# A Mamba mixer's groups: C computed a group ahead, states times C and gate sums on VectorE, the first z columns beside dt

## The chip, the cores and the metric

The kernel runs on one core of one Trainium2 chip. The metric is the device time of one execution in microseconds (us). The engines are named as in the profile: PE is TensorE (PEld its weight loads), DVE VectorE, ACT ScalarE, POOL GpSimd, and SP SyncE, which issues the DMAs. A name such as "SPq" means the instruction queue of that engine.

## The reference

One step of a decoder layer for 256 prompt tokens and 8 sample tokens, which bring their own recurrent states. All of it is float32.

```python
h = h + 0.5 * rmsnorm(swiglu(rmsnorm(h)))          # FFN 1
mix = token_mixer(rmsnorm(h))                      # the part that is changed
h = h + rmsnorm(mix)
h = h + 0.5 * rmsnorm(swiglu(rmsnorm(h)))          # FFN 2
h = h + rmsnorm(sigmoid(rmsnorm(h) @ w_ple_gate) * (p @ w_ple_proj))

def token_mixer(u):
    glu_a, glu_b, z, xbc, dt = split(u @ w_in)     # 1024, 1024, 3072, 5120, 48 columns
    v = silu(layernorm(dwconv31(glu_a * sigmoid(glu_b))))
    x, B, C = split(silu(dwconv4(xbc)))            # 3072, 8 x 128, 8 x 128
    dt = softplus(dt + dt_bias)                    # 48 heads, 6 in each of 8 groups
    a_cs = cumsum(dt * a)                          # per chunk of 128 tokens
    y = (C . B * exp(a_cs[l] - a_cs[s])) @ (x * dt)   # within a chunk
      + exp(a_cs) * (C @ state)                    # from the state before
      + d_skip * x
    y = y * silu(z)
    y = y * rsqrt(mean over the group's 384 columns of y * y + eps) * ssm_norm_g
    return concat(v, y) @ w_out                    # and the new states
```

For a sample token the chunk is that one token, so `C @ state` is the product of its own state, 128 numbers for each of 64 x 48 rows, with C, summed over the 128.

## The kernel before, in words

Columns of a projection lie on 128 partitions, the 264 tokens along the free axis. Each float32 weight is split into a high and a low part in TensorE's fast float32 form, and so is each activation; a 128 x 128 weight tile then gives three matmuls of 128x264 into one accumulator: high x high, high x low, low x high (`mm3`, L250 to L252).

**Weights** stream in units of up to 16 tiles (48 matmuls), in the order of a table (`PLAN`). A unit comes in two halves of eight tiles, 512 KB each. Per half, SP issues the load of `wraw` (L153), ACT casts it to `whi` (L154), and DVE subtracts to get `wlo` (L155). Each of the three tiles has four buffers, so two units; a half of unit n + 2 can be made only once PE has finished that half of unit n. A column unit of the input projection is one such unit: 128 output columns.

**The mixer's input projection** runs over 81 column units (`IN_ORDER`): first `dt`, then for each of 8 groups B, C, x0, (in four groups a pair for the GLU), x1, x2, z0, z1, z2. The first four units are computed together, so they end at one time.

After each B, C or x unit comes `do_conv`: a width-4 convolution on DVE (STTs, L219) and a SiLU on ACT (L243). After `dt`, `do_dt` writes dt and dt x a of the samples to memory (`d_dt`) and loads them back repeated over the partitions (`dtp`, `eap`), takes the exponential of `eap`, forms the running sums with matmuls and writes them to memory (`d_cs`).

`decays(g)`, at x0, loads the group's running sums from `d_cs` twice (`ab`, `ea`, L702 and L710) and makes the decays with 12 Relus and 3 exponentials on ACT. `ssd(g)`, at x2, does the scan of the group: PE transposes x and B (L727, L728), forms C . B (L741), the states (L753), the products within a chunk (L768) and from the state (L775). Then, for the samples, it transposes B and C (L781, L782), copies them to `rows` on ACT (L784), writes `d_bc`, loads C back repeated over all partitions as `cbc` (L787), and for each of the 3 x 2 pieces of the sample states loads `h0` (128 x 512, L792), multiplies it by `cbc` on GpSimd and sums it over the last axis on DVE (L794). GpSimd also scales the first chunk's state by `cd`.

`gate(g)`, at x0 of the next group, multiplies y by SiLU(z) and forms the sum of squares with `SumSq`: ACT squares, GpSimd adds (`run`), and a matmul with ones (L306) sums over the partitions. `L216` and `L219` are helpers for DVE and GpSimd operations, `L243` that for ACT's.

The order of the instructions on each engine is set by a scheduler when the program is built; each engine then works through its own in that order, and waits for the others at semaphores. The memory tiles `d_bc`, `d_cs` and `d_dt` make a write and a load that depends on it go through SP's queue one behind the other.

```python
rows = mp.tile([P, 2, P], F32, tag="rows", bufs=1, name=nm("rows"))
cbc = mp.tile([P, NS, P], F32, tag="cbc", bufs=1, name=nm("cbc"))
h0 = mp.tile([P, 4, P], F32, tag="h0", bufs=3, name=nm("h0"))
ab: bufs=2, one for each chunk;  ea: bufs=1
```

## Time and profile before

| | |
|---|---|
| median of 3 runs | 2429.63 us (2427.08 to 2433.99) |
| the profiled execution, its own time | 2432.44 us |
| its span | 2430.7 us |
| mean granted clock of TensorE | 0.993 |
| busy share PE, DVE, ACT, POOL | 97%, 65%, 49%, 12% |
| the mixer's input projection | about 820 to 1362 us of the span |
| bytes read from memory | 465.65 MB |

A row of the wait view reads: engine, tile and line that waited `<-` what it waited for: total us, times, longest. A row of the group view reads: line, engine, operation, out`<-`in, shapes, count | busy us, mean ns of one | idle time of the engine before them and what ended it. A row of the timeline or of the chain of work that ended last begins with start and duration; in square brackets is the idle time before it.

### The profile page before, as it was taken

The numbers are of one execution on the slowest core, as the hardware profiler recorded it, in microseconds if no ns is written. First come the engines' busy times: TensorE is split into PE (matmuls) and PEld (weight loads), VectorE is DVE, ScalarE is ACT, GpSimd is POOL, SyncE is SP. The second block draws the span as 40 slices with busy tenths as digits, with TensorE's granted clock in tenths as the row PEclk, the third lists the DMA queues.
The fourth block names the chain that finished last, engine by engine and source line by source line (L and its number), as shares of the span: only waits on it lengthen the run. The fifth ranks groups of instructions, "written<-read, shape, count | busy, mean of one in ns | idle before, by whom it ended". The sixth has DMA issues, their size and how long they took to land.

```text
span 2430.7 us, 47409 instructions
## 1 busy us (share of the span) xinstructions
PE 2367.7 (97%) x19448; PEld 2342.7 (96%) x19448; DVE 1569.2 (65%) x2333; ACT 1181.4 (49%) x1771; POOL 298.4 (12%) x295
## 2 busy tenths in 40 slices
PE   8999999999999889999999999999999999999988
PEld 8999999999999889999999999999999999999988
DVE  6554455545557858988798975766545565565585
ACT  6444444433456465665565545544444443344465
POOL 0400000000015212122122010101000000000103
PEclk9999999999999999999999999999999999999999
DMA  7655555555556666666666556476766776676553
GB/s 249 217 183 184 182 183 182 183 183 183 183 169 207 213 180 193 207 216 202 210 216 205 181 181 216 153 238 228 240 213 223 237 236 217 217 236 206 184 191 132
DMA packets 166250, 489.89 MB, mean 202 GB/s; under 512 B 25568, under 2 KB 42640, under 8 KB 166032
## 3 DMA queue, kind: packets, MB, share of 16 engines
q1 hardware_dynamic: 166032, 486.86, 62.0%
q8 instruction: 152, 2.49, 0.4%
q14 instruction: 66, 0.54, 0.1%
HBM read 465.65 MB, written 22.42 MB: 201 GB/s over the span
## 4 chain that ended last, share of the span: by engine, by line
PE 84%; DVE 6%; issue 3%; ACT 3%; DMA 2%; POOL 1%; SPq 0%; ACTq 0%; POOLq 0%; DVEq 0%
PE acc L250 27%; PE acc L251 27%; PE acc L252 27%; DVE wlo L155 2%; DVE y L219 1%; ACT whi L154 1%; PE ps L306 1%; DVE h L216 1%; DMA ab<-d_cs 1%; DMA cbc<-d_bc 1%; DVE ych L794 1%; PE ps L250 0%; ACT tmp L243 0%; DMA d_bc<-rows 0%; PE ps L251 0%
## 5 line engine op out<-in xcount | busy, mean ns | idle before, releaser
L252 PE MATMUL acc<-act,wlo 128*128 128x264 f32 x6224 | 1770.7, 285 | 4.3 <-DVE wlo L155 4.1
L251 PE MATMUL acc<-act,whi 128*128 128x264 f32 x6224 | 1756.6, 283 | 6.3 <-DVE act L216 6.2
L250 PE MATMUL acc<-act,whi 128*128 128x264 f32 x6224 | 1747.7, 283 | 3.4 <-DVE tmp L216 2.1
L155 DVE TENSOR_TENSOR wlo<-wraw,whi 128x1024 fp32r<-128x1024 f32 (+2 forms) x812 | 986.9, 1217 | 597.9 <-ACT whi L154 595.5
L154 ACT CAST whi<-wraw 128x1024 fp32r<-128x1024 f32 (+2 forms) x812 | 829.9, 1026 | 961.9 <-PE acc L251 717.3
L250 PEld LDWEIGHTS acc<-act,whi 128*128 128x128 f32 x6224 | 1175.5, 190 | 6.0 <-issue 2.1
L251 PEld LDWEIGHTS acc<-act,whi 128*128 128x128 f32 x6224 | 1169.2, 188 | 9.9 <-DVE act L216 7.9
L252 PEld LDWEIGHTS acc<-act,wlo 128*128 128x128 f32 x6224 | 1167.9, 188 | 8.3 <-DVE wlo L155 6.4
L216 POOL TENSOR_TENSOR run<-run,tmp 128x264 f32<-128x264 f32 x93 | 87.8, 944 | 962.9 <-ACT tmp L243 961.8
L216 POOL TENSOR_TENSOR s<-s,eap 128x1024 f32<-128x1024 f32 x24 | 48.8, 2035 | 630.4 <-DMA s<-in_hst 630.4
L219 DVE SCALAR_TENSOR_TENSOR y<-v,vec,y 128x251 f32<-128x251 f32 (+23 forms) x240 | 118.1, 512 | 1.2
L219 DVE SCALAR_TENSOR_TENSOR s<-bb,xds,s 128x128 f32<-128x128 f32 x192 | 52.7, 346 | 66.1 <-POOL s L216 66.1
L216 POOL TENSOR_TENSOR h<-h,cbc 128x512 f32<-128x512 f32 x48 | 73.6, 1553 | 166.0 <-DMA cbc<-d_bc 90.9
L258 ACT CAST act<-tmp 128x264 fp32r<-128x264 f32 x120 | 48.7, 410 | 69.9 <-DVE tmp L216 55.2
L216 DVE TENSOR_TENSOR tmp<-acc,rr 128x264 f32<-128x264 f32 x100 | 43.0, 430 | 51.0 <-PE acc L252 50.8
L216 DVE TENSOR_TENSOR tmp<-tmp,acc 128x264 f32<-128x264 f32 x86 | 36.7, 427 | 38.7 <-PE acc L252 38.6
L216 DVE TENSOR_TENSOR act<-tmp,act 128x264 fp32r<-128x264 f32 x120 | 56.1, 471 | 0.3
L243 ACT ACTIVATE tmp<-tmp 128x264 f32<-128x264 f32 x112 | 47.0, 420 | 8.7 <-DVE tmp L216 8.4
L243 ACT ACTIVATE tmp<-y 128x264 f32<-128x264 f32 x67 | 28.0, 425 | 44.1 <-DVE y L216 43.0
L216 DVE TENSOR_TENSOR y<-y,acc 128x264 f32<-128x264 f32 x80 | 34.0, 425 | 24.0 <-PE acc L252 24.0
L794 DVE TENSOR_REDUCE ych<-h 128x4 f32<-128x512 f32 x48 | 32.4, 678 | 17.5 <-POOL h L216 17.5
L250 PE MATMUL ps<-act,whi 128*128 128x264 f32 x96 | 28.4, 304 | 15.4 <-ACT whi L154 8.1
(165 smaller groups left out, 926.1 us busy)
## 6 DMA issues: line engine op xcount, KB each, us to landing
wraw<-in_w SPq DMA_DIRECT2D x756, 512.0 KB, 4.7
h<-in_hst SPq DMA_DIRECT2D x48, 256.0 KB, 3.9
s<-in_hst SPq DMA_DIRECT2D x24, 512.0 KB, 6.5
out_nss<-s SPq DMA_DIRECT2D x24, 512.0 KB, 3.0
wraw<-in_w SPq DMA_DIRECT2D x24, 384.0 KB, 4.1
wraw<-in_w SPq DMA_DIRECT2D x32, 256.0 KB, 3.9
ab<-d_cs SPq DMA_DIRECT2D x16, 384.0 KB, 5.1
cbc<-d_bc SPq DMA_DIRECT2D x8, 512.0 KB, 4.3
```

The lines of the kernel that those rows point to most:

```text
L154: nc.scalar.copy(hi, raw)
L155: nc.vector.tensor_tensor(out=lo, in0=raw, in1=hi.bitcast(F32), op=ALU.subtract)
L216: return (eng or nc.vector).tensor_tensor(out=out, in0=in0, in1=in1, op=op)
L219: return nc.vector.scalar_tensor_tensor(out=out, in0=in0, scalar=scalar, in1=in1, op0=op0, op1=op1)
L243: i = nc.scalar.activation(out=out, in_=in_, func=func, bias=bias, scale=scale)
L250: nc.tensor.matmul(acc, hi, x[:, 0, :], start=first, stop=False)
L251: nc.tensor.matmul(acc, hi, x[:, 1, :], start=False, stop=False)
L252: return nc.tensor.matmul(acc, lo, x[:, 0, :], start=False, stop=last).ins
L258: nc.scalar.copy(t[:, 0, :], x)
L306: nc.tensor.matmul(p, ones, s, start=i == 0, stop=i == len(self.parts) - 1)
L794: nc.vector.tensor_reduce(out=ych[:, j, b : b + 4], in_=h0, op=ALU.add, axis=AX.X)
```

## The change

It rearranges the mixer.

- The first four units are dt, z0, z1, z2 of group 0 (before: dt, B, C, x0). C of a group is computed in the group before it, behind x2. Group 0 runs z0, z1, z2, C0, B0, x0, x1, x2, C1; a later group B, x0, (pair), x1, x2, C of the next, z0, z1, z2.
- `do_dt` is split in four: `do_dt`, `do_sums` (at B of group 0), `do_exps` and `load_dt` (at x1). The exponential of dt x a is taken on 48 x 8 before the write instead of on the loaded, repeated 128 x 192.
- `load_sums` (loads of `ab`, `ea`) comes at B, the decays' ACT work at x1, tied behind the cast of the last weight half issued so far. `decay_cb` (C . B and its product with the decays) moves from x2 to x1.
- B and C each have a `b` and `c` tile and their own transposed copy to memory (`to_memory`), through a `rows` tile with one buffer, half the size.
- `h0` is one piece of 128 x 1024 (512 KB) per column tile, with two buffers. Its product with `cbc` and the sum run on DVE, one product and one reduce for each tile, tied behind the last weight subtract issued so far; at x0, x1, x2 of groups 2 to 7, and one unit later in groups 0 and 1.
- The product of the state with `cd` and the gate's additions run on DVE. The gate is split: `gate_begin` at B of the next group, `gate_end` with the matmul total at x0, tied behind the last matmul issued so far.
- The tiles `btm` and `cb` are taken from the `rr` tiles.

`tc.issue_after(i)` sets what follows behind instruction i in the order.

```diff
+        z = [("z", MT_Z + 3 * g + j) for j in range(3)]
+        if g == 0:
+            out.extend(z)
+            out.append(("C", MT_CM))
         out.append(("B", MT_BM + g))
-        out.append(("C", MT_CM + g))
         out.append(("x", MT_X + 3 * g))
         if g in GLU_IN:
             pair()
         out.extend(("x", MT_X + 3 * g + j) for j in (1, 2))
-        out.extend(("z", MT_Z + 3 * g + j) for j in range(3))
+        if g + 1 < GRP:
+            out.append(("C", MT_CM + g + 1))
+        if g:
+            out.extend(z)
...
+    def do_exps(dta):
+
+        act(dte, dte, AF.Exp)
+        act(cd, cd, AF.Exp)
+        ed = mp.tile([P, NS], F32, name="ed")
+        act(ed[:NH], dta[:, NP_:], AF.Exp)
+        nc.sync.dma_start(d_dt[1], ed[:NH])
...
-        act(eap, eap, AF.Exp)
...
+    def decays(g):
+
+        ab, ea = sums.pop(g)
+        with tc.issue_after(ws.hi):
+            for c, t in enumerate(ab):
+                for h in range(HPG):
+                    i = HPG * g + h
+                    act(t[:, h, :], t[:, h, :], AF.Relu, bias=acs[:, c, i : i + 1], scale=-1.0)
+                act(t, t, AF.Exp, scale=-1.0)
+            act(ea, ea, AF.Exp)
         return ab, ea
+
+    def to_memory(g, i, t):
+
+        pr = ps_tile([P, P])
+        nc.tensor.transpose(pr[:NS], t[:, NP_:], ident)
+        rows = mp.tile([P, P], F32, tag="rows", bufs=1, name=nm("rows"))
+        nc.scalar.copy(rows[:NS], pr[:NS])
+        nc.sync.dma_start(d_bc[g, i], rows[:NS])
+
+    def load_cbc(g):
+        cbcs[g] = mp.tile([P, NS, P], F32, tag="cbc", bufs=1, name=nm("cbc"))
+        with tc.issue_after(ws.dma.ins):
+            nc.sync.dma_start(cbcs[g], d_bc[g, 1].partition_broadcast(P))
+
+    def load_state(g, j):
+        h0s[g, j] = mp.tile([P, NS, P], F32, tag="h0", bufs=2, name=nm("h0"))
+        with tc.issue_after(ws.dma.ins):
+            nc.sync.dma_start(h0s[g, j], a["hst"][3 * g + j])
+
+    def state_times_c(g, j):
+
+        if not j:
+            ychs[g] = mp.tile([P, 3, NS], F32, tag="ych", bufs=1, name=nm("ych"))
+        h0 = h0s.pop((g, j))
+        with tc.issue_after(ws.lo):
+            tt(h0, h0, cbcs[g], ALU.mult)
+            nc.vector.tensor_reduce(out=ychs[g][:, j, :], in_=h0, op=ALU.add, axis=AX.X)
...
-                tt(s, states[0], cd[:, hs].unsqueeze(2).to_broadcast([P, HPG, 64]), ALU.mult, nc.gpsimd)
+                tt(s, states[0], cd[:, hs].unsqueeze(2).to_broadcast([P, HPG, 64]), ALU.mult)
...
-        for j in range(3):
-            for b in range(0, NS, 4):
-                h0 = mp.tile([P, 4, P], F32, tag="h0", bufs=3, name=nm("h0"))
-                nc.sync.dma_start(h0, a["hst"][3 * g + j][:, b : b + 4, :])
-                tt(h0, h0, cbc[:, b : b + 4, :], ALU.mult, nc.gpsimd)
-                nc.vector.tensor_reduce(out=ych[:, j, b : b + 4], in_=h0, op=ALU.add, axis=AX.X)
...
+    def gate_begin(g, y, zs):
+
         tt(y, y, zs, ALU.mult)
-        sq = SumSq(3, direct=0)
+        sq = SumSq(3, direct=0, eng=nc.vector)
         for j in range(3):
             sq.add(y[:, j, :])
+        return g, y, sq
+
+    def gate_end(g, y, sq):
+
         t = tmp()
-        rsqrt(t, sq.total(), eps1, 1.0 / 384)
+        rsqrt(t, sq.total(traced[0]), eps1, 1.0 / 384)
...
```

Three places where the order of instructions moves follow. A row there has the line, the operation, what it writes and reads, and the shape; the last number of a name is that of the tile.

TensorE at the gate total between groups 2 and 3, before: the total (L306) over `run`, and the transposes of x0 (L727), behind the first matmul of x1's unit.

```order
L252 MATMUL acc_12452<-act_9315,wlo_8_12336 128x264
L250 MATMUL acc_12514<-act_9201,whi_0_12392 128x264
L306 MATMUL ps_12035<-run_12026,ones 128x264
L727 MATMUL ps_12218<-ident,h_12017 128x128
L727 MATMUL ps_12227<-ident,h_12017 128x128
L251 MATMUL acc_12514<-act_9201,whi_0_12392 128x264
```

The same place after the change: the total (L316) stands behind all 48 matmuls of the unit `acc_12376`, which began with `wlo_0_12158`'s half, and C . B (L779) and the transposes (L795) follow it.

```order
L261 MATMUL acc_12376<-act_9315,wlo_8_12164 128x264
L316 MATMUL ps_12040<-run_11944,ones 128x264
L779 MATMUL ps_12146<-c_11656,b_11935 128x128 x2
L795 MATMUL ps_12229<-ident,h_12026 128x128
L261 MATMUL acc_12441<-act_9201,wlo_0_12304 128x264
```

What moved: the total's input `run` is now made on DVE, and the total is the first of the small matmuls there.

DVE in a group's second unit, before: the reduces (L794) of the state products stand one by one between convolution steps and weight subtracts (L155).

```order
L155 TENSOR_TENSOR wlo_8_11965<-wraw_8_11963,whi_8_11964 128x1024
L219 SCALAR_TENSOR_TENSOR bc_11874<-acc_11886,vec,bc_11874 128x253
L794 TENSOR_REDUCE ych_11574<-h_622_11579 128x4
L219 SCALAR_TENSOR_TENSOR h_12017<-acc_11956,vec,h_12017 128x255
L216 TENSOR_TENSOR h_12017<-h_12017,shist 128x8
L219 SCALAR_TENSOR_TENSOR y_11352<-v_11346,vec,y_11352 128x232
L794 TENSOR_REDUCE ych_11574<-h_623_11583 128x4
L155 TENSOR_TENSOR wlo_0_12080<-wraw_0_12078,whi_0_12079 128x1024
```

After, at the head of group 3 (`h_11518` is y, `h_11734` SiLU(z), `h_647` and `h_648` are sample states):

```order
L162 TENSOR_TENSOR wlo_8_12069<-wraw_8_12067,whi_8_12068 128x1024
L226 SCALAR_TENSOR_TENSOR y_11342<-v_11336,vec,y_11342 128x237
L223 TENSOR_TENSOR h_11518<-h_11518,h_11734 128x792
L223 TENSOR_TENSOR h_647_11959<-h_647_11959,cbc_11736 128x1024
L223 TENSOR_TENSOR h_648_11961<-h_648_11961,cbc_11736 128x1024
L226 SCALAR_TENSOR_TENSOR y_11342<-v_11336,vec,y_11342 128x236
L772 TENSOR_REDUCE ych_12034<-h_647_11959 128x8
L772 TENSOR_REDUCE ych_12034<-h_648_11961 128x8
L226 SCALAR_TENSOR_TENSOR y_11342<-v_11336,vec,y_11342 128x235
L226 SCALAR_TENSOR_TENSOR h_12026<-acc_12060,vec,h_12026 128x255
L223 TENSOR_TENSOR h_12026<-h_12026,shist 128x8
L162 TENSOR_TENSOR wlo_0_12158<-wraw_0_12156,whi_0_12157 128x1024
```

What moved: two products and two whole reduces stand together between two weight halves, and the first product reads `cbc_11736`. Right behind the last row comes the gate's addition, `run_11944`. SP's rows that bring this `cbc` (C's rows are `rows_11666`, B's of the group before `rows_11577`):

```order
L724 DMA ab_11953<-d_cs 128x6x128
L160 DMA wraw_0_12156<-in_w 128x1024
L751 DMA d_bc<-rows_11577 8x128
L727 DMA ea_11956<-d_cs 64x3x128 x2
L160 DMA wraw_8_12162<-in_w 128x1024
L751 DMA d_bc<-rows_11666 8x128
L758 DMA cbc_11736<-d_bc 128x1024
```

Before, there was one write of both (8x2x128), and the load of `cbc` behind it.

ACT in group 0, before: the exponential of the loaded `eap` stands ahead of the SiLUs of B, C (`bc`) and x0 (`h_9644`).

```order
L618 COPY tmp_9624<-ps_9621 48x256
L243 ACTIVATE eap<-eap 128x192
L243 ACTIVATE dte<-dte 128x96
L243 ACTIVATE cd<-ps_9612 128x48
L238 ACT_TABLE_LOAD
L243 ACTIVATE bc_9627<-bc_9627 128x264 x2
L243 ACTIVATE h_9644<-h_9644 128x264
```

After: the exponential is that of `ed`, 48 x 8; the Relus on the loaded `ab` stand between the casts of two halves of one weight unit.

```order
L250 ACTIVATE cd<-cd 128x48
L250 ACTIVATE ed<-h_9584 48x8
L161 CAST whi_8_9859<-wraw_8_9858 128x1024
L655 COPY xo_9667<-acc_9851 128x11
L250 ACTIVATE h_9836<-acc_9851,vec 128x264
L161 CAST whi_0_9961<-wraw_0_9960 128x1024
L250 ACTIVATE ab_9844<-ab_9844,acs 128x128 x6
L250 ACTIVATE ab_9845<-ab_9845,acs 128x128 x6
L161 CAST whi_8_9967<-wraw_8_9966 128x1024
```

What moved: ACT's wait for a load in this group is now that for `ab`, with the cast of a weight half behind it. SP's order there is: the write of `d_bc` (C's rows of group 0), a weight half, `cbc` load, a weight half, the write of `d_cs`, that of `d_dt`, then the loads of `ab`.

## Prediction

> **What bounds the kernel now.** I read the page's busy shares first, then busy time by stage, then TensorE's waits in the one stage that the change touches.

> ```profile
> PE 2367.7 (97%) x19448; PEld 2342.7 (96%) x19448; DVE 1569.2 (65%) x2333; ACT 1181.4 (49%) x1771; POOL 298.4 (12%) x295
> 200.00:700.00 500.00, 500.00 (x4169) 500.00 (x4168) 252.51 (x272) 204.78 (x246) 0.00 (x0) 1.00 0.58 182
> 820.00:1362.00 542.00, 517.17 (x4205) 499.84 (x4205) 441.95 (x759) 314.36 (x579) 99.91 (x75) 0.99 0.64 200
> ```

> TensorE is the bound. In the first FFN it never stops: 4169 matmuls in 500 us, 0.120 us each, so a unit of 48 takes 5.76 us (about 5.9 in the mixer with its small matmuls). In the mixer's input projection (820 to 1362 us; the columns are span, PE, PEld, DVE, ACT, POOL, granted clock, DMA share, GB/s) it is busy for 517 of 542 us, and DVE for 442. The change leaves TensorE's work as it is, so it can only win what TensorE loses here: idle time and clock.

> ```profile
> PE ps L306 <- POOL run L216: 11.8, 8, 2.6
> PE ps L727 <- ACT h L243: 7.3, 2, 4.9
> PE acc L252 <- DVE wlo L155: 4.1, 8, 0.9
> PE ps L753 <- ACT btm L736: 1.1, 1, 1.1
> ```

> These are TensorE's waits between 820 and 1362 us (total, times, longest). The eight gate totals wait for GpSimd's sum of squares, two stops come in group 0, and the late low halves of weights cost 4.1. Lost clock comes on top:

> ```profile
> 863.11 0.69 PE L727 MATMUL ps<-ident,h 128*128 128x128 f32 x2 [4.90 <-ACT h L243]
> 875.87 0.64 PE L727 MATMUL ps<-ident,h 128*128 128x128 f32 x3 [2.43 <-ACT h L243]
> 857.00:868.00 11.00, 6.10 (x39) 5.89 (x39) 1.59 (x3) 7.12 (x15) 0.00 (x0) 0.84 0.68 197
> 868.00:880.00 12.00, 9.57 (x66) 9.25 (x66) 9.15 (x15) 10.69 (x22) 0.00 (x0) 0.86 0.43 135
> 918.00:930.00 12.00, 9.43 (x64) 9.11 (x63) 8.32 (x16) 8.13 (x16) 2.95 (x2) 0.86 0.64 217
> ```

> The three windows around the 4.9, the 2.43 and the longest gate wait (2.6) show clocks of 0.84, 0.86 and 0.86: 0.16 x 11 + 0.14 x 12 + 0.14 x 12 = 5.1 us lost, 1.7 behind each gap.

> **The change, part by part.** The sum is made against the profiled execution, 2432.44 us (span 2430.7 and 1.7 around it). That one lies 2.8 above the median of the three runs, 2429.63, so 2.8 comes off at the end.

> *Gate totals, -11.8 and -1.7 of clock.* The sums of squares go to DVE one unit earlier, and the total is issued at the end of x0's unit. In the order shown, the last addition stands right behind `wlo_0_12158` on DVE, while TensorE has all 48 matmuls of that half's unit (5.8 us) ahead of the total. If the sum were late, the weights ahead of it would be later still. I take the whole wait as gone. What is late next at that place are the weights, priced below.

> *Group 0, -7.3 and -3.4 of clock, +4.7 back.*

> ```profile
> ACT eap L243 <- DMA eap<-d_dt: 7.7, 1, 7.7
> 843.50 4.51 DMA d_dt<-h
> 856.55 5.54 DMA d_cs<-tmp
> 862.11 3.98 DMA ab<-d_cs
> ```

> ACT stood 7.7 us for the reloaded `eap`, with the SiLU of x0 behind it, which TensorE's transposes need. After the change the exponential comes before the write and ACT doesn't wait for it. But the decays still need the running sums through memory: 5.54 to write `d_cs` and 3.98 to load `ab`, 9.5 in all. And SP now puts the B write and the `cbc` load, which waits for that write, ahead of `d_cs`. ACT's twelve Relus on `ab` stand between the casts of two halves of a weight unit, so a late `ab` holds back the second cast and the subtract and matmuls behind it. Bounds: 0, if z's three units of head start cover it, to the present 7.3 and 3.4. I take 3.0 of wait, the nearest gaps being 2.43 and 4.9, with 1.7 of clock.

> [...]

> *State times C, on DVE.*

> ```profile
> L155 DVE TENSOR_TENSOR wlo<-wraw,whi 128x1024 fp32r<-128x1024 f32 x173 | 212.0, 1225 | 200.6 <-ACT whi L154 200.6
> L155 DVE TENSOR_TENSOR wlo<-wraw,whi 128x1024 fp32r<-128x1024 f32 x156 | 197.9, 1272 | 49.2 <-ACT whi L154 48.3
> L794 DVE TENSOR_REDUCE ych<-h 128x4 f32<-128x512 f32 x48 | 32.4, 678 | 17.5 <-POOL h L216 17.5
> L216 DVE TENSOR_TENSOR tmp<-acc,rr 128x264 f32<-128x264 f32 x100 | 43.0, 430 | 51.0 <-PE acc L252 50.8
> L216 DVE TENSOR_TENSOR xdt<-ps,tm 128x384 f32<-128x384 f32 x16 | 8.3, 549 | 0.5 <-PE ps L728 0.5
> L216 DVE TENSOR_TENSOR h<-h,h 128x792 f32<-128x792 f32 x8 | 7.8, 977 | 0.1
> L216 POOL TENSOR_TENSOR h<-h,cbc 128x512 f32<-128x512 f32 x48 | 73.6, 1553 | 166.0 <-DMA cbc<-d_bc 90.9 <-DMA h<-in_hst 25.0 <-issue 17.6
> ```

> (The first row is the FFN's, the fourth the page's, the others are the mixer's.) GpSimd's 73.6 us of products become 24 DVE products of 128x1024. Priced as the same shape's subtract, 24 x 1.225 = 29.4. The reduces stay at 32.4: half as many, twice as long. Sixteen gate additions at 0.43 add 6.9, eight st x cd at 0.549 add 4.4. Together +40.7. Without GpSimd beside it the subtract should fall from 1.272 to the FFN's 1.225, -7.3 over 156. So DVE goes from 442 to about 475 of some 530 us, 90%: still under TensorE on average. The question is where it stands still.

> DVE works in order, and its first product of a group now waits for `cbc`; behind it stand the next weight halves. Before, GpSimd waited there at nobody's cost (90.9 us in the last row). When does `cbc` land?

> ```profile
> 1198.52 1.09 SPq L702 DMA_DIRECT2D ab<-d_cs  x2
> 1200.25 5.22 DMA d_bc<-rows
> 1205.49 3.70 DMA cbc<-d_bc
> 1021.65 0.29 SPq L785 DMA_DIRECT2D d_bc<-rows  x1
> 1023.97 0.56 SPq L787 DMA_DIRECT2D cbc<-d_bc  x1
> 953.43 6.09 DMA d_bc<-rows
> 959.58 4.47 DMA cbc<-d_bc
> ```

> From `ab`'s issue to the write of the rows 1.7 us; a write until the load that waits for it starts, 2.3 (1021.65 to 1023.97), 5.2 or 6.1; the load 3.7 or 4.5. After the change there are two writes in a row: the `rows` tile has one buffer, so C's copy waits until B's write has been confirmed. So `cbc` lands between 1.7 + 2 x 2.3 + 0.4 + 4.3 = 11.0 and 1.7 + 2 x 6.1 + 0.4 + 4.5 = 18.8 us after `ab`'s issue. I take 14.5, with the writes at the middle of these rows, a little over 4. DVE is there just under two units (11.8 us) after `ab`, say 11. It idles 3.5 us, in each of seven groups.

> How much of that reaches TensorE? A half's buffers come free 1.5 units (8.9 us) before its use. Cast (1.05) and subtract (1.2) leave 6.6. In the rows shown, between `wlo_8_12068` and `wlo_0_12158` stand y x z (0.98), two products (2.45), two reduces (2.7), three conv steps (some 1.5): 7.4 to 8. The buffers of two halves come free 3 us apart, so DVE falls 4.5 behind and 2.1 of 6.6 is left. Of 3.5 us, 1.4 shows on TensorE; over seven groups about 10, some of it where 4.1 was already lost: from 4.1 to 13, **+9**. Bounds: 0 where `cbc` lands at 11, 7 x (7.8 - 2.1) = 40 at 18.8.

> *What costs nothing.* Eight more row copies on ACT (under 0.4 us each) and the extra SP issues lie beside TensorE: ACT is busy for 314 of 542, and the bytes loaded are the same. If SP blocks long enough for a weight load to be late, the cast shows it; that is part of the upper bound above. The waits on `btm` (1.1) may stay.

> Sum: -11.8 - 1.7 - 10.7 + 4.7 + 9 = -10.5: 2432.4 becomes 2421.9, and 2.8 off gives **2419**.

> **The rivals.** *A: `cbc` is in time.* At 11 us after `ab` DVE does not stop, and the 9 falls away: 2410, and 2405 if group 0's wait is covered too. For it: the 2.3 us write. Against: writes of 5.2 and 6.1 in other groups, and queueing behind weight loads. [...]

> *B: the new wait costs more than the old ones.* Place: DVE's first product of each group. If `cbc` lands 17 us after `ab`, 6 us of idle less 2.1 of cover is 3.9, x 7 = 27; two gaps over 2.4 us cost 3.4 of clock. -24.2 + 4.7 + 27 + 3.4 = +10.9, so **2440**, slower. It decides from -24.2 + 4.7 = -19.5 on, 2.8 per group: `cbc` at 16 us. For it: 5.2 and 6.1 fit that. Against: all seven groups would have to be slow.

> *C: group 0 wins nothing.* `ab` is as late as `eap` was, and the 7.3 and 3.4 stay. Then -13.5 + 9 = -4.5: 2425, no change that counts. For it: the same 9.5 us through memory, behind one more blocked load; against: three z units of room.

> *D: the gate totals stay late*, since DVE's additions stand behind the products: 11.8 back, 2431. The position behind `wlo` speaks against it.

> **How the numbers follow.** About 0.3% (7.3 us) is what a measurement of this kernel can tell from no change: faster is below 2422.3, slower above 2436.9. Forecast (2412 to 2424) 0.47, A 0.20, C 0.17, B 0.12, D 0.04. Faster: 0.42 of the forecast, A, 0.03 of C: 0.65. Slower: 0.08 of B's 0.12. Same: the rest, 0.27. The range takes in A with both gains, and of B what lies up to 16.6 us for `cbc`: 2405 to 2436. Below it is about 0.06, above it 0.09.

> **What would show it.** Right: no wait of TensorE on the gate total; POOL empty in the groups; a DVE row that waits for `cbc` seven times, some 3 us each; TensorE's waits on `wlo` at 10 to 16 us; one stop of 2 to 4 us in group 0, with a low clock behind it, beginning at ACT's `ab`. Waits on `wlo` under 6 mean A, over 25 mean B; a stop in group 0 over 5 means C; waits on the total mean D. It would be wrong in kind if TensorE waited for something not priced here: small matmuls behind a late DVE (L779, L795, L812) or a cast behind a late weight load.

## The result

The changed kernel takes 2407.33 us (median of 4 runs, 2406.94 to 2408.97), the kernel before 2431.58 in the same comparison: a ratio of 0.9905, with a 95% interval of 0.9888 to 0.9921. That is faster, by some 23 us by the ratio, and the gain is larger than forecast (2419, 10.5 off the profiled execution). The profiled execution took 2407.66 us, 24.8 less than the one before, with a span of 2405.9. The number lies in the range, at its lower end, outside the band of the forecast itself (2412 to 2424), between rival A's 2405 and 2410. The waits on `wlo` under 6 us, A's sign, say the same.

The page's busy shares, for the changed kernel:

```profile
PE 2360.8 (98%) x19448; PEld 2339.3 (97%) x19448; DVE 1574.2 (65%) x2357; ACT 1185.1 (49%) x1780; POOL 201.5 (8%) x223
```

Its busy time in the mixer's input projection and in group 0 (columns as before: span, PE, PEld, DVE, ACT, POOL, clock, DMA share, GB/s):

```profile
820.00:1340.00 520.00, 514.40 (x4237) 500.64 (x4237) 457.18 (x804) 319.53 (x590) 2.38 (x3) 1.00 0.66 212
840.00:900.00 60.00, 57.36 (x461) 54.99 (x460) 43.15 (x73) 34.41 (x65) 0.00 (x0) 0.97 0.72 219
```

TensorE's waits from 800 to 1345 us (total, times, longest):

```profile
PE acc L260 <- DVE act L223: 3.3, 4, 1.6
PE ps L795 <- ACT h L250: 2.1, 1, 2.1
PE acc L261 <- DVE wlo L162: 2.0, 3, 1.1
PE ps L316 <- DVE run L223: 0.9, 1, 0.9
PE ps L812 <- DVE xde L223: 0.3, 1, 0.3
```

The first wait lies ahead of the input projection and was there before. The gate totals cost 0.9 instead of 11.8, group 0 one stop of 2.1 instead of 7.3, and the late low halves 2.0 instead of 4.1: forecast had been 13. So the changed kernel's waits come to 5.3, against 24.7 before. DVE is busy for 457 of 520 us (88%; some 90% had been forecast), and still TensorE hardly waits for it. DVE's own wait for `cbc` in the same stretch, and its three largest groups of one shape in the mixer:

```profile
DVE h L223 <- DMA cbc<-d_bc: 11.6, 8, 2.3
```

```profile
L162 DVE TENSOR_TENSOR wlo<-wraw,whi 128x1024 fp32r<-128x1024 f32 x167 | 203.2, 1220 | 33.4 <-ACT whi L161 31.0 <-PE acc L260 1.7
L223 DVE TENSOR_TENSOR h<-h,cbc 128x1024 f32<-128x1024 f32 x24 | 29.2, 1221 | 11.6 <-DMA cbc<-d_bc 11.6
L772 DVE TENSOR_REDUCE ych<-h 128x8 f32<-128x1024 f32 x24 | 29.0, 1213 | 0.1
```

The new wait on `cbc` is there, at the place that was forecast, but it comes to 11.6 us in eight groups, the longest 2.3, and not 3.5 in each of seven.

Counted between the same two matmuls, near 820 us and at the stage's end, the input projection took 545.3 us before and 519.4 after; the rest of the span is 1885.4 and 1886.6 us, and 1884 to 1888 in every kernel below. So all that follows is about this stage.

### The profile page after: what moved, and what is told of

The parts are those of the page before. It is cut to its first block, busy times and chain, and to the rows that moved or that the text cites. A ratio compares the mean times of both kernels' runs of the same rounds, so it can differ in the third digit from the quotient of the medians.

```text
span 2405.9 us, 47285 instructions
## 1 busy us (share of the span) xinstructions
PE 2360.8 (98%) x19448; PEld 2339.3 (97%) x19448; DVE 1574.2 (65%) x2357; ACT 1185.1 (49%) x1780; POOL 201.5 (8%) x223
## 4 chain that ended last, share of the span: by engine, by line
PE 92%; DVE 3%; ACT 2%; issue 2%; DMA 1%; POOL 0%; SPq 0%; ACTq 0%; DVEq 0%; POOLq 0%
PE acc L259 29%; PE acc L260 29%; PE acc L261 29%; ACT whi L161 1%; DVE wlo L162 1%; PE ps L259 1%; PE ps L316 1%; PE ps L260 1%; PE ps L261 0%; DMA wraw<-in_w 0%; PE ps L827 0%; DVE tmp L226 0%; PE ps L812 0%; DVE act L223 0%; DVE h L223 0%
## 5 line engine op out<-in xcount | busy, mean ns | idle before, releaser
L223 POOL TENSOR_TENSOR run<-run,tmp 128x264 f32<-128x264 f32 x77 | 71.5, 929 | 897.7 <-ACT tmp L250 897.2
L226 DVE SCALAR_TENSOR_TENSOR y<-v,vec,y 128x247 f32<-128x247 f32 (+24 forms) x240 | 106.7, 468 | 0.6
L223 POOL TENSOR_TENSOR run<-run,y 128x264 f32<-128x264 f32 x7 | 7.1, 1013 | 572.9 <-ACT run L303 495.0
L259 PE MATMUL ps<-act,whi 128*128 128x264 f32 x96 | 28.3, 303 | 16.6 <-ACT whi L161 9.3
L223 DVE TENSOR_TENSOR h<-h,cbc 128x1024 f32<-128x1024 f32 x24 | 29.2, 1221 | 11.6 <-DMA cbc<-d_bc 11.6
```

Of the source, the lines that this page charges most:

```text
L223: return (eng or nc.vector).tensor_tensor(out=out, in0=in0, in1=in1, op=op)
L226: return nc.vector.scalar_tensor_tensor(out=out, in0=in0, scalar=scalar, in1=in1, op0=op0, op1=op1)
L259: nc.tensor.matmul(acc, hi, x[:, 0, :], start=first, stop=False)
```

## The experiments

Two questions were open. Why did the new wait on DVE cost nothing? And which part of the change brought the gain? Eight kernels start from the changed one (a part taken back, the new wait pushed either way, group 0 ordered otherwise), four do one part alone in the kernel before. The median of each stands beside its ratio to the kernel before, which ran along on the same chip (2428.4 to 2429.5 there), with the interval.

| kernel | us | ratio to before |
|---|---|---|
| the change | 2407.33 | 0.9905 (0.9888 to 0.9921) |
| B's rows written early | 2405.17 | 0.9898 (0.9883 to 0.9912) |
| one more write ahead of cbc | 2427.81 | 0.9988 (0.9976 to 0.9999) |
| two more writes | 2433.86 | 1.0016 (1.0007 to 1.0025) |
| products on GpSimd | 2423.15 | 0.9967 (0.9956 to 0.9979) |
| gate's additions on GpSimd | 2409.83 | 0.9925 (0.9907 to 0.9943) |
| group 0's z behind C1 | 2411.88 | 0.9936 (0.9916 to 0.9956) |
| running sums ahead of cbc | 2403.73 | 0.9897 (0.9882 to 0.9912) |
| this and B's rows early | 2404.20 | 0.9900 (0.9885 to 0.9915) |
| before, gate's additions on VectorE | 2426.28 | 0.9991 (0.9981 to 1.0002) |
| before, gate split and early | 2427.79 | 0.9999 (0.9990 to 1.0009) |
| before, exponential ahead of the write | 2431.41 | 1.0011 (1.0002 to 1.0020) |
| before, products on VectorE | 2443.00 | 1.0061 (1.0044 to 1.0078) |

**How much can VectorE wait for cbc?** First an edit that frees the `rows` tile earlier, so that `cbc` waits for one write instead of two:

```diff
     def ssd_samples(g, bf, cf, xt, y):
-        to_memory(g, 0, bf)
...
             if j == 1:
+                to_memory(g, 0, bcs[g, 0])
                 decay_cb(bcs[g, 0], bcs[g, 1], ab)
```

> The changed kernel with B's rows written out at x1 instead of after x2, so that the rows tile is free when C's rows come and the cbc load waits for one write instead of two. Theory 1 (VectorE's wait for cbc is hidden by the slack of the weight halves): that wait falls from 11.6 us in 8 to under 5, and the time stays within 3 us of the changed kernel's 2407. Theory 2 (that wait is passed on to TensorE): some 7 to 9 us faster, about 2399.

The wait didn't fall. It rose, from 11.6 to 20.1 us, as DVE's waits show, and the timeline of group 6 shows one of them (start, duration, in brackets the idle time before):

```profile
DVE h L223 <- DMA cbc<-d_bc: 20.1, 8, 4.2
```

```profile
1180.97 0.97 SPq L724 DMA_DIRECT2D ab<-d_cs  x2
1193.49 1.23 DVE L223 TENSOR_TENSOR h<-h,cbc 128x1024 f32<-128x1024 f32 x1 [4.13 <-DMA cbc<-d_bc]
```

`ab` is issued at 1180.97 and the first product starts at 1193.49, 12.5 us later, with DVE idle 4.13 us ahead of it. `cbc` came somewhat earlier (products 11.3 to 12.9 us after `ab` in groups 1 to 7), DVE earlier still. TensorE's waits on `wlo` stayed at 2.0 and the time didn't change within the intervals. The edit failed at what it was for, and answers the question all the same: a stop of DVE of 4.1 us at this place can cost nothing.

Then the other way, a write and a wait on SP's queue put between:

```diff
         with tc.issue_after(ws.dma.ins):
-            nc.sync.dma_start(cbcs[g], d_bc[g, 1].partition_broadcast(P))
+            nc.sync.dma_start(d_bx[g], d_bc[g, 1])
+            nc.sync.dma_start(cbcs[g], d_bx[g].partition_broadcast(P))
```

> The changed kernel with one more write to memory and wait on SyncE's queue between C's rows and the cbc load, some 4 us later in each group. VectorE's wait for cbc should grow from 1.3 to some 5 us in each of seven groups. Theory 1 with the prediction's cover of 2.1 us per group: 7 x 3 = 21 us slower, about 2428, all of it TensorE's waits on wlo. Theory 2 (passed on one to one): 28 us slower, 2435. Theory 3 (the cover is larger than the prediction had it, 5 us or more): under 6 us slower, below 2413.

> The same with two more writes, some 8 us later. Theory 1 with 2.1 of cover: 7 x 7 = 49 us slower, 2456. Theory 3 with a cover of 5 or more: 7 x 4 = 28 or less, 2435 or below. Between this run and the one with one write the slope should be one to one in every theory: about 28 us.

With one more write, the waits of TensorE and DVE, the timeline of group 5, and the busy time around its stop:

```profile
PE acc L261 <- DVE wlo L162: 13.4, 6, 4.7
DVE h L223 <- DMA cbc<-d_bx: 26.5, 8, 5.0
```

```profile
1134.89 0.97 SPq L725 DMA_DIRECT2D ab<-d_cs  x2
1153.27 2.36 DVE L223 TENSOR_TENSOR h<-h,cbc 128x1024 f32<-128x1024 f32 x2 [4.97 <-DMA cbc<-d_bx]
1160.27 0.59 PE L261 MATMUL acc<-act,wlo 128*128 128x264 f32 x1 [4.74 <-DVE wlo L162]
```

```profile
1155.00:1175.00 20.00, 15.26 (x107) 14.99 (x106) 20.00 (x35) 7.97 (x12) 0.00 (x0) 0.83 0.58 186
```

In group 5 the first product starts 18.4 us after `ab`, and behind it TensorE has to stop for 4.74 us, until 1160.27, on a low half; the clock around it is 0.83. Over all groups the waits on `wlo` grow from 2.0 to 13.4, the stop in group 0 from 2.1 to 3.5, and the mean clock of the execution falls from 0.995 to 0.991, which is some 10 us of 2420. Added up that is 23 us, more than there is: the ratios 0.9905 and 0.9988 lie 20 us apart, the two profiled executions 17.1. The parts overlap to some extent: in group 5 the low clock begins 1.8 us before the stop ends.

The starts of the first product after `ab`'s issue, read from the same two rows of each of groups 1 to 7, tell roughly where the cover ends. The change: 11.3 to 14.9, and no wait on `wlo` until 33 us after `ab`. One more write: 14.1 to 18.4, with none at 14.1, 15.0 and 16.9, and then 1.5 us at 15.3, 2.5 at 16.7, 3.5 at 17.1 and 4.7 at 18.4. Two more: 15.9 to 21.6, with none at 19.0, 2.2 us at 21.6, and the longest, 4.9, at 18.7. So the cover is no single number, and a late product isn't passed on at a fixed rate.

What differs between groups is where the next weight subtract stands behind the first product. DVE's rows in groups 3 and 5 of the change:

```profile
1023.23 2.36 DVE L223 TENSOR_TENSOR h<-h,cbc 128x1024 f32<-128x1024 f32 x2 [0.26 <-DMA cbc<-d_bc]
1028.97 1.22 DVE L162 TENSOR_TENSOR wlo<-wraw,whi 128x1024 fp32r<-128x1024 f32 x1
1139.24 1.22 DVE L223 TENSOR_TENSOR h<-h,cbc 128x1024 f32<-128x1024 f32 x1 [1.05 <-DMA cbc<-d_bc]
1141.48 1.22 DVE L162 TENSOR_TENSOR wlo<-wraw,whi 128x1024 fp32r<-128x1024 f32 x1
```

In group 3 both products and both reduces come first, and the subtract starts 5.7 us behind the first product; in the other six groups it starts 1.1 to 4.2 us behind it. Its half was ready just when TensorE needed it in group 3, and 1.7 to 4.4 us ahead in the others. With one more write the three longest stops are those of groups 3, 5 and 7, where the subtract starts 5.3 to 5.7 us behind. In groups 5 and 7 that is a new order (2.2 and 1.9 in the change): the edit moved DVE's order along with the load, so these stops aren't the price of the later load alone.

The time agrees with the first theory's 2428, but not for its reason: the waits on `wlo` grew by 11 us and not by 21, and a part of the loss is clock. With two writes another 6 us are lost, not 28: `cbc` is issued 3.9 us later after `ab` on the mean (14.7 instead of 10.9), but the first products start only 2.5 us later (18.7 instead of 16.2). Why the load then takes less time stays open.

**The products' engine.**

```diff
-            tt(h0, h0, cbcs[g], ALU.mult)
+            tt(h0, h0, cbcs[g], ALU.mult, nc.gpsimd)
```

> The changed kernel with the 24 products of state and cbc (128x1024) back on GpSimd, the reduces still on VectorE. VectorE loses 29 us of work, GpSimd gets some 24 x 3.1 = 74 us, and VectorE waits for GpSimd's product before the first reduce. If moving the products to VectorE bought the gain (GpSimd stretches VectorE's instructions beside it), wlo gets late again: 4 to 15 us slower, and wlo's mean rises from 1.207 towards 1.27 in the mixer. If the product's engine does not matter: within 3 us of 2407.

TensorE's waits in this kernel, and the groups of DVE and GpSimd that matter:

```profile
PE ps L316 <- DVE run L223: 6.4, 2, 3.5
PE acc L261 <- DVE wlo L162: 5.6, 6, 1.6
```

```profile
L162 DVE TENSOR_TENSOR wlo<-wraw,whi 128x1024 fp32r<-128x1024 f32 x161 | 212.7, 1322 | 44.0 <-ACT whi L161 43.5 <-PE acc L260 0.2
L223 POOL TENSOR_TENSOR h<-h,cbc 128x1024 f32<-128x1024 f32 x24 | 61.0, 2556 | 406.0 <-DMA cbc<-d_bc 315.3 <-DVE h L226 56.9 <-DMA h<-in_hst 18.5
```

DVE lost 29 us of products and the kernel got 15 us slower. The subtracts beside GpSimd take 1.322 us on the mean instead of 1.220, 16 us over 161, and DVE waits 17.3 us in five places for GpSimd's products; the additions of the gate behind them are late too, and the total waits again. In the stage TensorE's waits rise by 11 us and the low clock (0.993 over the execution instead of 0.995) costs some 5 more, which is about all of it. So the products do belong on DVE, once they are early.

But only then. In the kernel before, at their old place:

```diff
-                tt(h0, h0, cbc[:, b : b + 4, :], ALU.mult, nc.gpsimd)
+                tt(h0, h0, cbc[:, b : b + 4, :], ALU.mult)
```

> The kernel before with the 48 products of 128x512 on VectorE, at their old place. VectorE gets 48 x 0.65 = 31 us and the stretched instructions go (wlo from 1.272 towards 1.22), but now VectorE stands still until cbc lands where GpSimd did. If the products' place, ahead of the group, is what makes VectorE bear them: TensorE's waits on wlo grow from 4 to over 10, and the time is the same as before or slower. If VectorE without GpSimd beside it was the gain: 3 to 8 us faster.

Four of TensorE's waits between 820 and 1362 us, the two longest among them:

```profile
PE ps L727 <- ACT h L243: 9.2, 3, 5.1
PE ps L753 <- DVE xde L216: 6.0, 3, 2.9
PE ps L306 <- POOL run L216: 1.5, 1, 1.5
PE acc L252 <- DVE wlo L155: 1.3, 2, 0.9
```

15 us slower. `wlo` is not late (1.3) and its mean does fall, to 1.223, so the expectation had the wrong victim: DVE's stops for `cbc` (16.8 us) now delay what stands in its queue beside the weights, `xde`, which the states' matmuls need, and more. All of TensorE's waits in the stage come to 29, only 4.5 more than before. The larger part is clock: 0.97 in this stage instead of 0.99, some 10 us. The wait on the gate total is down to 1.5 here, but the sum comes no earlier: it ends 3.6 to 5.0 us after the start of y times SiLU(z) (3.5 to 4.9 before), and TensorE now gets to the total later.

**The gate: engine or place?** The change moves the additions to DVE and a unit ahead. One kernel undoes the engine alone (the first edit), one does it alone in the kernel before (the second), and one does the place alone there (the third):

```diff
-        sq = SumSq(3, direct=0, eng=nc.vector)
+        sq = SumSq(3, direct=0)
```

```diff
-        sq = SumSq(3, direct=0)
+        sq = SumSq(3, direct=0, eng=nc.vector)
```

```diff
-    def gate(g, y, zs):
+    def gate_begin(g, y, zs):
...
+        return g, y, sq
+
+    def gate_end(g, y, sq):
         t = tmp()
-        rsqrt(t, sq.total(), eps1, 1.0 / 384)
+        rsqrt(t, sq.total(traced[0]), eps1, 1.0 / 384)
...
             do_conv(acc, m - MT_X, bct[:, 0, :])
+            if pend:
+                gated.append(gate_begin(*pend.pop()))
```

> The changed kernel with the gate's 16 additions back on GpSimd; the place of gate_begin and gate_end stays. If the place (a unit earlier, total behind the x0 unit) removed the wait of 11.8 us: within 2 us of the changed kernel, wait on the total under 2. If the engine did: some 8 to 12 us slower.

> The kernel before with only the gate's additions moved to VectorE, at their old place. If the engine is what matters: 8 to 13 us faster than before. If the place is: the wait on the total stays near 11.8, now for VectorE, and the time within 4 us of before.

> The kernel before with the gate split as in the change, gate_begin at B of the next group and the total behind x0's unit, the additions still on GpSimd. If the place is what removed the wait on the gate total (11.8 us): that wait under 2 us, 8 to 13 us faster than before. If it needs VectorE too: under 4 us faster.

TensorE's waits from 820 to 1362 us: both that the changed kernel with GpSimd's additions has, and that on the total in the other two, in this order:

```profile
PE acc L261 <- DVE wlo L162: 4.4, 5, 3.2
PE ps L795 <- ACT h L250: 2.1, 1, 2.1
```

```profile
PE ps L306 <- DVE run L216: 9.1, 8, 1.8
```

```profile
PE ps L309 <- POOL run L216: 11.6, 8, 2.3
```

With the place of the change, GpSimd's additions do: no wait on the total at all, and the time is 2 to 5 us above the change's (by median and by ratio), with intervals that overlap. The engine alone wins 2.7 of 11.8, and a time that the interval doesn't tell from no change. The surprise is the third: the code of the gate stands two units earlier there, and nothing moved. The timelines say why: GpSimd's and DVE's in the kernel before (ahead of the total at 1175.2), then DVE's with the gate split (total at 1170.2):

```profile
1156.57 2.54 POOL L216 TENSOR_TENSOR h<-h,cbc 128x512 f32<-128x512 f32 x2 [4.25 <-DMA h<-in_hst]
1168.57 0.18 DVE L216 TENSOR_TENSOR h<-ych,sy 128x24 f32<-128x24 f32 x1
1170.26 0.98 DVE L216 TENSOR_TENSOR h<-h,h 128x792 f32<-128x792 f32 x1
1172.15 3.02 POOL L216 TENSOR_TENSOR run<-run,tmp 128x264 f32<-128x264 f32 x2 [13.05 <-ACT tmp L243]
```

```profile
1163.52 0.18 DVE L216 TENSOR_TENSOR h<-ych,sy 128x24 f32<-128x24 f32 x1
1165.21 0.98 DVE L216 TENSOR_TENSOR h<-h,h 128x792 f32<-128x792 f32 x1
```

y times SiLU(z), the 128x792 row, reads the samples' part of y, the 128x24 row, and that is the end of the state products: six of them on GpSimd until 1159.1, then reduces and four small steps on DVE, each queued between weight subtracts. In both kernels the gate begins 1.7 us behind this row and 5 us before its total. Splitting it can't move it. In the kernel with the additions on GpSimd and the rest of the change, the same product starts at 1132.91, for a total at 1139.7.

**Group 0.** The exponential alone in the kernel before:

```diff
-        nc.sync.dma_start(d_dt[1], dta[:, NP_:])
+        ed = mp.tile([P, NS], F32, name="ed")
+        act(ed[:NH], dta[:, NP_:], AF.Exp)
+        nc.sync.dma_start(d_dt[1], ed[:NH])
...
-        act(eap, eap, AF.Exp)
```

> The kernel before with one part of the change alone: the exponential of dt x a on 48 x 8 before it is written, none on the loaded eap. If ScalarE's 7.7 us wait for eap caused TensorE's two stops in group 0 (7.3 us and 3.4 of clock): 5 to 10 us faster than before. If ScalarE then waits for ab at the same place (the running sums come through memory as late): under 3 us faster.

The change with group 0's z units behind C1:

```diff
         if g == 0:
-            out.extend(z)
             out.append(("C", MT_CM))
...
-        if g:
-            out.extend(z)
+        out.extend(z)
```

> The changed kernel with z0 to z2 of group 0 behind C1, as in the other groups, so that dt, C0, B0, x0 are the first four units. Theory (the head start of the z units covers the sums' way through memory): group 0 loses 7 to 12 us again, in waits of TensorE around 860 to 890 and in clock, 2414 to 2419. Rival (taking the exponential before the write did it, the z units are not needed): within 3 us of 2407.

And the change with group 0's load of `cbc` tied behind the write of the running sums:

```diff
-        nc.sync.dma_start(d_cs, cs[:, :NP_])
+        sums["dma"] = nc.sync.dma_start(d_cs, cs[:, :NP_]).ins
...
-        with tc.issue_after(ws.dma.ins):
+        with tc.issue_after(ws.dma.ins if g else sums["dma"]):
             nc.sync.dma_start(cbcs[g], d_bc[g, 1].partition_broadcast(P))
```

> The changed kernel with group 0's cbc load behind the write of the running sums on SyncE's queue, where it was ahead of it. The write could go at 847.6 instead of 850.3 us. If the block by the cbc load caused the 5.5 us wait of ScalarE on ab: that wait falls by 2 to 3 us, TensorE's 2.1 us wait and the low clock behind it go, 3 to 4 us faster, about 2403.5. If a weight load ahead of it holds SyncE's queue as long: no change.

With the exponential ahead of the write ScalarE's wait moves from `eap` to `ab`, nearly as long as it was, and TensorE stops once instead of twice, for 7.7 us instead of 7.3 in all. Nothing is won (1.0011). The waits of the two from 835 to 900 us and from 820 to 1362 us:

```profile
ACT ab L243 <- DMA ab<-d_cs: 7.4, 2, 7.1
PE ps L728 <- ACT h L243: 7.7, 1, 7.7
```

Busy time from 840 to 900 us, first with z behind C1, then with the running sums ahead of `cbc`, of which SP's timeline and ScalarE's wait follow:

```profile
840.00:900.00 60.00, 55.25 (x426) 52.47 (x425) 40.58 (x65) 31.23 (x61) 0.00 (x0) 0.94 0.70 209
```

```profile
840.00:900.00 60.00, 59.21 (x489) 56.85 (x489) 44.46 (x73) 36.50 (x72) 0.00 (x0) 1.00 0.73 227
```

```profile
847.05 0.32 SPq L617 DMA_DIRECT2D d_cs<-tmp  x1
851.76 0.97 SPq L724 DMA_DIRECT2D ab<-d_cs  x2
```

```profile
ACT ab L250 <- DMA ab<-d_cs: 3.3, 1, 3.3
```

Without the head start of the z units TensorE is busy 55.25 us there instead of 57.36, at a clock of 0.94 instead of 0.97: some 4 us, between the two expectations. So z gives a part of group 0's gain. The running sums are written at 856.55 us before, at 853.42 without the head start and at 850.29 in the change, so half of their lead is z's. The rest of the gain comes with the other half and the exponential together, which weren't taken apart further. In the last kernel the running sums are written at 847.05 instead of 850.29 and `ab` is issued at 851.76 instead of 855.03; ScalarE's wait falls from 5.5 to 3.3, TensorE's stop to 0.6, and the clock is 1.00. Its 2403.73 are 3.6 below the change's median (2 by the ratios). The intervals of the two ratios overlap, but the trace shows where these microseconds went: 1.5 of stop and 1.7 of clock. It is the fastest kernel here, and B's rows written early add nothing to it:

> The changed kernel with group 0's cbc load behind the write of the running sums and with B's rows written at x1, the two edits that were no slower. If their gains are separate (the first alone 0.9897 of before, the second 0.9898, the change 0.9905): about 0.989, 2402. If the second edit's 2 us were chance: as the first alone, 2403.7.

## Why the prediction was right, and where its sum was off

**Gate totals, -11.8 and -1.7: right in size** (0.9 left), and the place on DVE was read rightly. But it was put down to the addition's engine and its earlier unit. Neither engine (-2) nor split (0) brings it alone. By the timelines, what allowed the earlier unit is the early state product; no kernel has that product early with the gate left as it was, so this is read and not tested.

**Group 0, -10.7 and +4.7 back: right.** The forecast stop at the transposes behind ScalarE's wait for `ab` came, 2.1 us instead of 3.0. The clock of 0.97 from 840 to 900 is 1.8 us more, 1.7 had been taken. So 3.9 came back.

**State times C, +9: the step that failed.** It had DVE at its first product 11 us after `ab`, `cbc` at 14.5, a stop of 3.5, and 2.1 of it covered. The first product started 11.3 to 14.9 us after `ab`, 13.4 on the mean, and DVE had been idle for 1.3. So `cbc` came 1.1 earlier than taken and DVE 1.0 later. The cover was sized from the rows of group 3, the only order shown, and taken for all seven groups; group 3 is the tightest of them, with nothing left at 13.0 us after `ab` (13.1 by the prediction), while the others had 1.7 us and more left on the same half at up to 14.9. All three were off to the same side. In place of +9, the term was -2.1 (4.1 to 2.0). So the result is rival A's (0.20), and the right call of faster owes something to luck: the main term had the wrong sign. And A's reason, the short write of 2.3 us, didn't hold: in group 7 the first write held the second up for over 5 us again. From the chain of work that ended last:

```profile
1244.88 5.10 DMA d_bc<-rows
1250.36 1.20 DMA d_bc<-rows
1251.58 5.29 DMA cbc<-d_bc
```

Where rival B begins came out near: it decides at `cbc` 16 us after `ab` by the prediction, and with one more write, 16.2 on the mean, nearly all of the gain is gone (0.9988). But its sum doesn't hold: it had 19.5 us of waits at that point, and they grew by 11.4, the clock taking much of the rest.

**DVE's work: right.** Products 29.2 (29.4 forecast), the subtract 1.220 (1.225), reduces 29.0 (32.4).

**The ledger.** Waits 24.7 to 5.3 is 19.4; the clock, 5.1 to 1.8, is 3.3. The stage is 25.9 shorter (545.3 to 519.4), so 3.2 more came within what the profile counts as TensorE's busy time. From where stays open.

## What to carry to other kernels

A part of a change that only moves code earlier gains nothing while its input is late: look first for what its first instruction reads, and what stands directly ahead of it on its engine. Here the four parts tried alone gave -2, 0, +3 and +15 us, and the whole change -23. A wait on an in-order engine is to be priced by when the work behind it is needed, not by how long the engine is idle: 4.1 us of idle cost nothing in one kernel, and 3.3 us stood ahead of a stop of 3.5 in another. Where that work stands differs from group to group, so read the order of each group before one is taken for all.

## What was not expected of the hardware

In the changed kernel a gap of 2.13 us (at 867.91, with one of 0.5 some 3 us ahead of it) was followed by slow matmuls. The timeline of TensorE, whose second number is the duration:

```profile
867.91 0.44 PE L795 MATMUL ps<-ident,h 128*128 128x128 f32 x2 [2.13 <-ACT h L250]
868.61 0.42 PE L259 MATMUL acc<-act,whi 128*128 128x264 f32 x1
868.83 0.42 PE L260 MATMUL acc<-act,whi 128*128 128x264 f32 x1
```

The slow ones start every 0.22 us instead of 0.12, so this stop cost nearly twice its length: 2.13 us, and 1.7 more for the 3.42 us at 0.50 behind it. In the prediction's rows the shortest such gap was 2.43.

Not each such gap does it: the wait of 2.3 us ahead of the total at 1175.2 in the kernel before was not followed by a lower clock. The clock records tell the two apart. The low stretches in the traces of the kernel before and of the change are 3.41 or 6.83 us long (but for the last, which the end cuts off), and they start whole multiples of 3.413 us apart (862.90, 876.56 and 924.34 in the kernel before: 4 and 14 steps). On this grid, the stretch with the gap and the next one, first in the change, then before:

```profile
865.04:868.45 3.41, 1.28 (x9) 1.06 (x10) 3.41 (x6) 3.38 (x5) 0.00 (x0) 1.00 1.00 398
868.45:871.87 3.42, 3.42 (x18) 3.42 (x17) 3.42 (x4) 2.76 (x5) 0.00 (x0) 0.50 0.50 162
1173.49:1176.91 3.42, 1.68 (x12) 1.56 (x13) 2.35 (x2) 1.94 (x4) 1.69 (x1) 1.00 0.84 279
1176.91:1180.32 3.41, 3.41 (x30) 3.41 (x30) 1.96 (x5) 3.39 (x6) 0.00 (x0) 1.00 0.68 237
```
